# Attention over every 64th key: the order of the first four loads (Q block 0, keys, Q block 1, values)

## The chip, the cores and the metric

One core of one Trainium2 chip. Before the change: 130.33 us (130.28 to 130.64, 3 runs).

Names: PE is the matmul engine, ACT, DVE and POOL the three elementwise engines, SP the engine that issues the DMA transfers. A *piece* is one record of the trace that says when one of the 16 DMA engines moved one batch of bytes (256 bytes in the keys and values, 32 KB in the loads of Q, 8 KB in the stores), and how long that took. "Q 0" is short for Q block 0.

## The reference

```python
def setup_inputs():
    batch, heads, seq, dim = (8, 12, 1024, 64)      # Q, K, V: float32; stride: 64
def reference(Q, K, V, stride):
    scale = 1.0 / np.sqrt(dim)
    for i in range(seq):
        attend_positions = np.arange(0, seq, stride)            # 16 keys per head
        scores = np.einsum('bhqd,bhkd->bhqk', q, k) * scale
        weights = softmax(scores)                               # (shortened)
        result[:, :, i, :] = np.einsum('bhqk,bhkd->bhqd', weights, v)[:, :, 0, :]
```

Every query attends to the same 16 keys of its head. Q and the result are 25 MB each; the keys and values that are needed are 0.39 MB each, in rows of 256 bytes.

## The kernel before

The 96 heads are handled in 24 groups of 4. A group is one 1 MB load of Q, 16 transposes on PE with two copies on ACT, the scores, two exponentials on ACT, the sums and outputs on PE, a scaling on DVE, and one 1 MB store. Eleven Q buffers and nine output buffers let loads run far ahead of compute, and stores lag far behind it. All loads and stores are issued by SP on one queue:

```python
    nc.sync.dma_start(k_raw, _ap_with(K, kv_src))      # 1536 rows of 256 bytes
    nc.sync.dma_start(v_raw, _ap_with(V, kv_src))      # 1536 rows of 256 bytes
    ...
    def load(g):                                       # own form of the copy instruction
        qn[g] = qn_pool.tile([P, 32 * D], FP32, name="qn", tag="qn")
        _copy(nc, qn[g], _ap_with(Q, [[HG * SD // 32, 32], [1, HG * SD // 32]], g * HG * SD))
    for g in range(QBUFS):                             # QBUFS = 11
        load(g)
    ...
    nc.gpsimd.tensor_copy(out=v_bf, in_=v_raw)         # POOL, waits for the values
    ...
    for n in range(2):                                 # four value matmuls on PE;
        for c in range(2):                             # DVE spreads each into v_bd
            ...
    for g in range(2):                                 # PE: only now the first transposes
        for x in range(2):
            transposes(g, x)
    scores(0)
    for g in range(NG):
        ...                                            # sums, outputs, next scores and transposes
        store(g)
        if g + QBUFS < NG:
            load(g + QBUFS)
```

In PE's program order the transposes of Q block 0 stand behind the value matmuls, whenever Q block 0 arrives: in the trace of before it has landed at 8.8 us, and its first transpose starts at 14.29 us, after the last value matmul at 14.02.

The softmax here doesn't subtract the row's maximum and nothing guards it: scores larger than these inputs give would overflow.

## Time and profile before

| | before |
|---|---|
| time | 130.33 us |
| span of the profile | 128.5 us |
| DMA queue: first piece, last piece ended | 1.84, 127.08 us |
| compute: last instruction ended | 114.2 us |
| store 0 issued / first piece moved | 25.2 / 33.05 us |

The lines of the profile page that say what bounds the kernel: the span; the busy share of the DMA engines and the rate in 40 slices of 3.2 us; the DMA queue's packets, MB and share of 16 engines' time; and the shares of the chain of waits.

```profile
span 128.5 us, 2215 instructions
...
DMA  2999989999899899999999999999998999999980
GB/s 57 351 398 418 449 367 490 388 423 439 339 421 487 357 441 439 413 434 449 383 467 426 393 459 428 393 469 421 405 469 357 416 434 416 421 428 421 434 337 23
...
q1 hardware_dynamic: 7712, 51.12, 96.3%
...
ACT 60%; PE 13%; DVE 5%; DMA 3%; POOL 3%; issue 2%; ACTq 1%; DVEq 0%; POOLq 0%
```

The DMA share is 9 tenths or more from the second slice to the last but one, apart from single eights: the queue is the limit. The chain of waits names ACT, but that chain ends with the last compute instruction at 114.2 us; after that SP only waits for stores. The waits of SP (total us, times, longest us) show that end:

```profile
SPq L307 <- DMA out_dram<-out_sb: 12.6, 1, 12.6
```

The start, from the timeline (start, duration, engine, line, what, and in brackets the idle time before and who ended it):

```profile
0.73 0.44 SPq L89 DMA_DIRECT2D k_raw<-in_K_dram  x1
...
1.23 0.71 SPq L90 DMA_DIRECT2D v_raw<-in_V_dram  x1
...
1.99 12.62 SPq L34 DMA_DIRECT2D qn<-in_Q_dram  x11
...
5.06 1.60 POOL L116 CAST k_dup<-k_raw 128x768 bf16<-128x768 f32 x2 [3.04 <-DMA k_raw<-in_K_dram]
...
7.80 0.83 POOL L124 CAST v_bf<-v_raw 128x768 bf16<-128x768 f32 x1
...
14.29 1.91 PE L193 MATMUL qt_ps<-identity,qn 128*128 128x128 bf16 x16
...
25.18 0.63 SPq L34 DMA_DIRECT2D out_dram<-out_sb  x1
```

The keys' POOL cast starts at 5.06 us, the values' at 7.80, the first transpose at 14.29, and store 0 is issued at 25.18. The trace's pieces show one stream: keys and values from 1.84 to about 6 us, then Q blocks 0 to 10 back to back, then store 0 at 33.05. Between the issue of store 0 and its turn lie almost 8 us: compute has slack.

### The profile page before, as it was taken

The page shows a single profiled execution, that of the slowest core. Times are in us where ns is not written, and L with a number is a line of the kernel's source. Part 1 is how long each engine was busy: PE and PEld are TensorE (multiplying, and loading weights), DVE is VectorE, ACT ScalarE, POOL GpSimd, SP SyncE. Part 2 cuts the span into 40 slices and gives each one's busy share as a digit, 9 for nine tenths or more (in the row PEclk, how much of TensorE's full clock was granted, in tenths as well). Part 3 has the DMA queues.
Part 4 walks back from the last instruction along what each step waited for, and adds up shares of the span by engine and source line. Part 5 has one row for each costly group of instructions (what it writes and reads, how often), then busy time and mean ns, then how long its engine had stood idle before and what let it go on. Part 6 is the DMA issues. An engine that isn't in the chain of part 4 may idle for free.

```text
span 128.5 us, 2215 instructions
## 1 busy us (share of the span) xinstructions
PE 69.4 (54%) x880; PEld 51.1 (40%) x880; DVE 83.7 (65%) x144; ACT 86.3 (67%) x103; POOL 5.1 (4%) x23
## 2 busy tenths in 40 slices
PE   0071665975656866558766578665687655510000
PEld 0040542754445654445544456443465444300000
DVE  6229963787677777787777877877877778750000
ACT  2163294988889888898888898888988888400000
POOL 4470000000000000000000000000000000000000
PEclk9999997799999999999999999999999999955555
DMA  2999989999899899999999999999998999999980
GB/s 57 351 398 418 449 367 490 388 423 439 339 421 487 357 441 439 413 434 449 383 467 426 393 459 428 393 469 421 405 469 357 416 434 416 421 428 421 434 337 23
DMA packets 7722, 51.26 MB, mean 399 GB/s; under 512 B 3872, under 2 KB 3872, under 8 KB 3872
## 3 DMA queue, kind: packets, MB, share of 16 engines
q1 hardware_dynamic: 7712, 51.12, 96.3%
q8 instruction: 7, 0.11, 0.4%
q14 instruction: 3, 0.02, 0.0%
HBM read 25.95 MB, written 25.17 MB: 398 GB/s over the span
## 4 chain that ended last, share of the span: by engine, by line
ACT 60%; PE 13%; DVE 5%; DMA 3%; POOL 3%; issue 2%; ACTq 1%; DVEq 0%; POOLq 0%
ACT qt L198 34%; ACT w L218 26%; PE sc L206 8%; DVE v_bd L180 3%; DMA k_raw<-in_K_dram 3%; PE qt_ps L193 2%; PE o_ps L238 2%; DVE out_sb L243 1%; POOL k_dup L116 1%; POOL perm_v L120 1%; PE sm L227 1%; POOL v_bf L124 1%; ACTq L307 1%; DVEq L307 0%; PE vp L175 0%
## 5 line engine op out<-in xcount | busy, mean ns | idle before, releaser
L243 DVE TENSOR_TENSOR out_sb<-o_ps,rec 128x512 f32<-128x512 f32 x96 | 63.3, 688 | 15.3 <-PE o_ps L238 12.9
L198 ACT COPY qt<-qt_ps 128x1024 bf16<-128x1024 bf16 x48 | 46.2, 1015 | 5.2 <-PE qt_ps L193 4.7
L218 ACT ACTIVATE w<-sc 64x512 bf16<-64x512 f32 x48 | 35.4, 737 | 13.2 <-PE sc L206 12.9
L238 PE MATMUL o_ps<-v_bd,w 128*128 128x256 bf16 x192 | 33.4, 278 | 0.6 <-DVE out_sb L243 0.6
L193 PE MATMUL qt_ps<-identity,qn 128*128 128x128 bf16 x384 | 30.7, 227 | 0.2 <-ACT qt L198 0.2
L193 PEld LDWEIGHTS <-qn 128*128 128x128 bf16 x384 | 27.0, 102 | 3.9 <-issue 2.6
L206 PE MATMUL sc<-qt,k_t 128*32 128x512 bf16 x96 | 9.8, 395 | 24.5 <-ACT qt L198 24.5
L238 PEld LDWEIGHTS <-w 128*128 128x128 bf16 x192 | 14.3, 98 | 6.9 <-issue 6.2
L206 PEld LDWEIGHTS <-k_t 128*32 128x32 bf16 x96 | 4.4, 93 | 29.3 <-issue 29.2
L231 DVE RECIPROCAL rec<-sm 128x32 f32<-128x32 f32 x24 | 8.6, 358 | 9.0 <-PE sm L227 9.0
L227 PE MATMUL sm<-s_sel,w 128*128 128x4 bf16 x192 | 8.5, 166 | 6.9 <-ACT w L218 6.9
L227 PEld LDWEIGHTS <-w 128*128 128x128 bf16 x192 | 6.4, 96 | 11.0 <-ACT w L218 11.0
L180 DVE TENSOR_SCALAR v_bd<-vp,mask 128x384 bf16<-128x384 f32 x16 | 8.5, 608 | 0.1
L166 ACT CAST k_t<-kp 64x512 bf16<-64x512 f32 x6 | 3.5, 579 | 3.6 <-PE kp L160 3.5
L160 PE MATMUL kp<-perm_k,k_dup 128*128 128x128 bf16 x12 | 1.5, 312 | 6.7 <-POOL k_dup L116 6.7
L175 PE MATMUL vp<-v_bf,perm_v 128*128 128x384 bf16 x4 | 1.8, 490 | 4.6 <-DVE v_bd L180 4.1
L160 PEld LDWEIGHTS <-k_dup 128*128 128x128 bf16 x12 | 1.2, 145 | 6.7 <-POOL k_dup L116 6.7
L138 DVE TENSOR_SCALAR slot_i<-iota_p 128x1 int16<-128x1 int16 x1 | 0.2, 156 | 4.7 <-POOL iota_p L136 4.7
L166 ACT ACT_TABLE_LOAD x1 | 1.3, 1283 | 2.5 <-DVE k_t L127 2.5
L127 DVE MEMSET k_t<- 128x1536 uint32 x1 | 1.3, 1338 | 1.1 <-PEq L293 1.1
L175 PEld LDWEIGHTS <-perm_v 128*128 128x128 bf16 x4 | 0.5, 127 | 3.7 <-issue 3.7
L116 POOL CAST k_dup<-k_raw 128x768 bf16<-128x768 f32 x2 | 1.6, 827 | 3.0 <-DMA k_raw<-in_K_dram 3.0
(15 smaller groups left out, 6.0 us busy)
## 6 DMA issues: line engine op xcount, KB each, us to landing
qn<-in_Q_dram SPq DMA_DIRECT2D x24, 1024.0 KB, 19.0
out_dram<-out_sb SPq DMA_DIRECT2D x24, 1024.0 KB, 19.5
k_raw<-in_K_dram SPq DMA_DIRECT2D x1, 384.0 KB, 4.3
v_raw<-in_V_dram SPq DMA_DIRECT2D x1, 384.0 KB, 5.4
```

Of the source, the lines that this page charges most:

```text
L116: nc.gpsimd.tensor_copy(out=k_dup[:, :, e], in_=k_raw)
L160: nc.tensor.matmul(kp[:, i], lhsT=k_dup[:, 4 * n + i].rearrange("p e d -> p (e d)"), rhs=pk, start=True, stop=True,)
L166: nc.scalar.copy(k_t[h, 4 * n : 4 * n + 4, :, :, e].rearrange("p n c s k -> p (n c s) k"), kp[h].rearrange("p n c s k -> p (n c s) k"),)
L180: nc.vector.tensor_scalar(out=v_bd[:, 6 * n : 6 * n + 6, c, s], in0=vp, scalar1=mask[:, s : s + 1], scalar2=None, op0=ALU.mult,)
L193: nc.tensor.transpose(ps[:, i], _ap_with(qb, [qb.ap[0], [2, P]], extra_offset=(8 * x + i) * 2 * P + 1), identity,)
L198: nc.scalar.copy(qt[g][:, x], ps)
L206: nc.tensor.matmul(sc[32 * j : 32 * j + 32], lhsT=kt[:, 32 * j : 32 * j + 32], rhs=_ap_with(q, [q.ap[0], [P, 8], [8 * P, 2], [1, 32]], ext ...
L218: nc.scalar.activation(out=_ap_with(wa, [wa.ap[0], [P, 8], [1, 2], [2, 32]], extra_offset=64 * a), in_=sc[64 * a : 64 * a + 64].rearrange( ...
L227: nc.tensor.matmul(sm[:, :, i], lhsT=wt[g][:, i], rhs=s_sel, start=True, stop=True)
L231: nc.vector.reciprocal(rec[g], sm.rearrange("p b i e -> p b (i e)"))
L238: nc.tensor.matmul(ps[:, :, i], lhsT=wt[g][:, 2 * c + i], rhs=v_bd[:, g // 2, g % 2].rearrange("p s d -> p (s d)"), start=True, stop=True,)
L243: nc.vector.tensor_tensor(out=out_sb[g][:, :, 4 * c : 4 * c + 4], in0=ps.rearrange("p b i (e d) -> p b (i e) d", e=2), in1=rec[g][:, :, 4 ...
```

## The change

Its intent is to have Q block 0 on the chip sooner, since compute starts with it. No byte and no instruction is added; only the order of SP's first four loads changes.

```diff
--- before.py
+++ after.py
@@ -86,8 +86,6 @@
     k_raw = const.tile([P, NC, D], FP32, name="k_raw")
     v_raw = const.tile([P, NC, D], FP32, name="v_raw")
     kv_src = [[stride * D, P], [2 * HG * SD, NC], [1, D]]
-    nc.sync.dma_start(k_raw, _ap_with(K, kv_src))
-    nc.sync.dma_start(v_raw, _ap_with(V, kv_src))
 
     qn = {}
 
@@ -99,6 +97,10 @@
 
     for g in range(QBUFS):
         load(g)
+        if g == 0:
+            nc.sync.dma_start(k_raw, _ap_with(K, kv_src))
+        elif g == 1:
+            nc.sync.dma_start(v_raw, _ap_with(V, kv_src))
 
 
     identity = const.tile([P, P], BF16, name="identity")
```

## The prediction

> **What bounds the kernel now.** The DMA queue, not an engine. By the DMA share per slice and the one-microsecond windows, the 16 DMA engines are full from about 3 us to 124 us; the queue table gives 96.3%. The transfer records show one first-in-first-out stream: keys and values (256-byte pieces) move from 1.84 to 6.05 us, Q block 0 lands at about 8.8 us, Q blocks 0 to 10 are followed at once by store 0, which begins at 33.05 us, and the last piece of store 23 ends at 127.1 us of the 128.5 us span. This agrees with the Trainium skill, "DMA: Bandwidth & Descriptors", section "Queues, rings and completion order": each engine consumes its ring in order.
>
> Compute is a second, shorter chain. The chain of waits says ACT 60%, but that chain ends at 114.2 us. In it ACT runs without a gap from 26 to 110 us, about 3.94 us a group, never waiting for Q. The last 12.6 us is SP waiting for stores.
>
> **What the change does.** It adds and removes no bytes and no instruction: on PE, DVE, ACT and POOL the order is the same, only SP's first four loads are permuted. On the queue Q 0 goes before the keys, Q 0 and Q 1 before the values. The intent, Q sooner, gains nothing: PE reads Q 0 first at 14.3 us, 5 us after it landed, because in PE's program order the transposes stand behind the four value matmuls, the last of which waits for DVE's v_bd (9.68 to 14.0 us).
>
> Costs (estimates from these durations): a Q block moves in 2.48 us (spacing of Q starts), keys or values in about 2. Keys should land near 7.5 us instead of 5.0, values near 11.7 instead of 6.6. The POOL cast of the values (now at 7.80) then starts near 11.8: +4.0 us. Everything behind it, v_bd, transposes, first exponential, store 0, moves by that: store 0 from 25.2 to about 29.2 us, end of compute from 114.2 to about 118.2.
>
> **On the critical path.** Almost nothing. The queue holds loads until 33.05 us, so store 0 issued at 29.2 (about 1.1 us from issue to first piece) comes in time; slack today is about 6.7 us, about 2.7 would be left. At the end store 23 would be issued near 118.3 and its turn comes at 122.3. The DMA stream stays gapless and ends at the same time. A small gain is possible: the first half of the keys took 1.4 us against 0.7 for later equal pieces; Q 0 in front may hide this. The final wait of SP should shrink from 12.6 to about 8.6 us.
>
> **Predicted:** 130.1 us, range 129.4 to 131.0 (8 in 10). Chances: faster by over 2% 0.02, within 2% 0.94, slower by over 2% 0.04.
>
> **What would show each step.** Right: K lands 2 to 3 us and V 4.5 to 5.5 us later; the first transpose near 18.3 us; store 0 issued near 29 us; DMA share still 0.9 or more in the slices from 26 to 36 us; last compute near 118 us; span 127.7 to 129. Wrong: a slice under 0.8 around 30 to 36 us would mean that the slack was used up.
>
> **What would make it wrong.** The small key and value pieces could move slower when mixed between the 32 KB pieces, delaying values by more than 6.7 us in all and opening a hole in the stream before store 0; or the one DMA engine that finishes 2 us after the others (127.1 against 125) may lag more or less.

## More of the kernel before

The metric is the device time of one execution in microseconds (us); a kernel's time is the median of its runs.

The view in stretches (length, busy time of each engine, PE clock, DMA share, GB/s; each piece is counted whole where it starts; one round of 16 pieces of 32 KB more or less at an edge is 33 GB/s in a stretch of 16 us, and 7 GB/s in one of 80 us):

```profile
core 0: us, PE busy (x) PEld busy (x) DVE busy (x) ACT busy (x) POOL busy (x), PEclk, DMA share, GB/s
0.00:16.00 16.00, 4.71 (x32) 3.47 (x33) 9.78 (x21) 5.37 (x8) 5.08 (x23) 1.00 0.94 334
16.00:32.00 16.00, 11.20 (x130) 8.03 (x128) 10.89 (x20) 12.73 (x16) 0.00 (x0) 0.89 1.01 421
32.00:112.00 80.00, 53.08 (x718) 39.52 (x719) 60.85 (x103) 68.16 (x81) 0.00 (x0) 1.00 1.00 422
112.00:128.50 16.50, 0.38 (x2) 0.10 (x1) 2.23 (x4) 0.00 (x0) 0.00 (x0) 0.53 0.79 330
```

From 16 to 112 us the stream runs at 421 to 422 GB/s; slower are only the opening and the last stretch, in which the stores run out. The Trainium skill, "HBM Reference", section "Specifications (TRN2)", says that a core which streams alone reaches about 425 GB/s; this trace agrees.

## The result, and the profile after

The changed kernel takes 131.13 us (130.95 to 131.39, 6 runs) against 130.51 us of before (130.28 to 130.64, 6 runs): ratio 1.0053, 95% interval 1.0038 to 1.0067. (Ratios here are the mean time of one kernel's fast runs over that of the other's of the same rounds, so not quite the ratio of the medians.) Run once more later, it came to 131.26 us, ratio 1.0069 (1.0056 to 1.0082). It is slower by a little, and clearly so: 131.13 lies just outside the predicted range of 129.4 to 131.0.

The page after:

```profile
span 129.2 us, 2215 instructions
...
DMA  5799999999899899999999999999999999999970
GB/s 162 234 388 373 426 446 426 386 426 421 360 444 467 375 444 446 388 449 431 393 472 426 388 467 411 406 467 391 421 441 391 413 429 416 434 416 431 413 330 23
...
q1 hardware_dynamic: 7712, 51.12, 96.2%
...
ACT 59%; PE 14%; DVE 5%; DMA 5%; issue 4%; POOL 2%; POOLq 1%; ACTq 1%; DVEq 0%; SPq 0%
```

The middle is as full as before, and there is no hole near 33 us, where store 0 comes in. The timeline of the start:

```profile
0.74 0.58 SPq L34 DMA_DIRECT2D qn<-in_Q_dram  x1
...
1.37 0.56 SPq L101 DMA_DIRECT2D k_raw<-in_K_dram  x1
1.99 0.93 SPq L34 DMA_DIRECT2D qn<-in_Q_dram  x1
...
2.96 0.59 SPq L103 DMA_DIRECT2D v_raw<-in_V_dram  x1
3.60 11.72 SPq L34 DMA_DIRECT2D qn<-in_Q_dram  x9
8.07 1.60 POOL L118 CAST k_dup<-k_raw 128x768 bf16<-128x768 f32 x2 [6.05 <-DMA k_raw<-in_K_dram]
...
12.40 0.83 POOL L126 CAST v_bf<-v_raw 128x768 bf16<-128x768 f32 x1 [1.52 <-DMA v_raw<-in_V_dram]
...
18.90 1.91 PE L195 MATMUL qt_ps<-identity,qn 128*128 128x128 bf16 x16
...
29.84 0.63 SPq L34 DMA_DIRECT2D out_dram<-out_sb  x1
...
30.57 0.55 SPq L34 DMA_DIRECT2D qn<-in_Q_dram  x1
```

The casts of keys and values start 3.0 and 4.6 us later (8.07 and 12.40 instead of 5.06 and 7.80), the first transpose 4.6 us later, store 0 was issued at 29.84 instead of 25.18, and compute ended near 119.2 instead of 114.2 us. (The values themselves landed 5.7 us later, at about 12.4 instead of 6.6 us; before, their cast stood behind other POOL work when they came.) SP's last wait shrank by nearly as much, as it should if late compute costs nothing:

```profile
SPq L309 <- DMA out_dram<-out_sb: 8.4, 1, 8.4
```

The stretches say where the time went:

```profile
0.00:16.00 16.00, 2.26 (x14) 1.55 (x15) 5.18 (x12) 4.76 (x7) 5.16 (x23) 1.00 0.92 313
16.00:32.00 16.00, 11.64 (x97) 8.03 (x97) 11.49 (x22) 9.05 (x11) 0.00 (x0) 1.00 1.01 423
32.00:112.00 80.00, 54.05 (x739) 40.64 (x737) 61.32 (x102) 69.20 (x83) 0.00 (x0) 1.00 1.00 423
112.00:128.50 16.50, 3.10 (x36) 1.84 (x36) 5.85 (x11) 3.30 (x4) 0.00 (x0) 0.75 0.82 343
```

From 16 to 112 us the rate is that of before (423 and 423 against 421 and 422 GB/s). The first 16 us are not: 313 GB/s instead of 334. Part of that gap is the edge at 16 us. With each piece spread evenly over its own duration the rates are 300 and 315 GB/s, and the difference, 0.24 MB, is 0.56 us of the later stream. What is missing there is moved at the end (343 instead of 330 in the last stretch).

The pieces give the same in time. The columns are the start of the first piece, the mean start of the 32 pieces of Q block 3 (by then keys, values and Q blocks 0 to 2 are through in either order), the mean start of the 128 pieces of store 23, and the end of the last piece, all in us:

```
                 first   Q block 3   store 23   last end
before            1.84     14.01      123.76     127.08
changed           2.10     14.57      124.32     127.74
difference       +0.27     +0.56       +0.56      +0.66
```

The stream is 0.56 us behind when Q block 3 starts, and as much at store 23, 110 us later. The loss happens in the opening of the stream and is never won back, since the stream has no gap in which it could be.

### The profile page after: what moved, and what is told of

It is laid out like the page before. It is cut to its first block, busy times and chain, and to the rows that moved or that the text cites. A ratio compares the mean times of both kernels' runs of the same rounds, so it can differ in the third digit from the quotient of the medians.

```text
span 129.2 us, 2215 instructions
## 1 busy us (share of the span) xinstructions
PE 71.1 (55%) x880; PEld 52.1 (40%) x880; DVE 83.8 (65%) x144; ACT 86.3 (67%) x103; POOL 5.2 (4%) x23
## 4 chain that ended last, share of the span: by engine, by line
ACT 59%; PE 14%; DVE 5%; DMA 5%; issue 4%; POOL 2%; POOLq 1%; ACTq 1%; DVEq 0%; SPq 0%
ACT qt L200 33%; ACT w L220 26%; PE sc L208 8%; DMA k_raw<-in_K_dram 5%; DVE v_bd L182 3%; PE qt_ps L195 3%; PE o_ps L240 2%; DVE out_sb L245 1%; POOL k_dup L118 1%; POOL perm_v L122 1%; PE sm L229 1%; POOLq L309 1%; ACTq L309 1%; DVEq L309 0%; SPq L34 0%
## 5 line engine op out<-in xcount | busy, mean ns | idle before, releaser
L240 PE MATMUL o_ps<-v_bd,w 128*128 128x256 bf16 x192 | 33.9, 281 | 0.6 <-DVE out_sb L245 0.6
L195 PE MATMUL qt_ps<-identity,qn 128*128 128x128 bf16 x384 | 31.6, 231 | 0.2 <-ACT qt L200 0.2
L195 PEld LDWEIGHTS <-qn 128*128 128x128 bf16 x384 | 27.6, 104 | 3.9 <-issue 2.6
```

Of the source, the lines that this page charges most:

```text
L195: nc.tensor.transpose(ps[:, i], _ap_with(qb, [qb.ap[0], [2, P]], extra_offset=(8 * x + i) * 2 * P + 1), identity,)
L240: nc.tensor.matmul(ps[:, :, i], lhsT=wt[g][:, 2 * c + i], rhs=v_bd[:, g // 2, g % 2].rearrange("p s d -> p (s d)"), start=True, stop=True,)
```

## The experiments

Three theories. **A**: what comes first in the stream sets the loss; opening with Q is dearer than opening with keys. **B**: each change between 256-byte and 32 KB pieces costs something; before has one such change, the changed kernel four. **C**: late compute costs it after all, at store 0 or at the last stores. Eleven runs were made, all correct. Each ratio is against runs of the kernel before on the same chip.

### e1: keys, Q 0, values, Q 1

```diff
-    nc.sync.dma_start(v_raw, _ap_with(V, kv_src))
 ...
         load(g)
+        if g == 0:
+            nc.sync.dma_start(v_raw, _ap_with(V, kv_src))
```

> Order keys, Q 0, values, Q 1: the keys open the stream as before, only the values are moved. Theory A (the loss of about 0.6 us is the opening of the stream by a 32 KB piece instead of 256-byte pieces): time within 0.15 us of before (ratio 1.000 to 1.001), first piece at 1.84 us. Theory B (the loss is paid at each change between small and large pieces; before has 1 change, the changed kernel 4, this one 3): about +0.4 us, ratio 1.003.

Measured: 130.70 us against 130.58, ratio 1.001 (0.999 to 1.003). Its first stretch:

```profile
0.00:16.00 16.00, 2.78 (x16) 1.70 (x17) 7.85 (x17) 4.76 (x7) 5.17 (x23) 1.00 0.92 334
```

334 GB/s, as before; Q block 3's pieces start at 14.00 us on the mean (before: 14.01). Three changes between large and small pieces cost nothing that can be seen. That speaks against B.

### e2 and e3: Q 0, keys, values, Q 1, and Q 0, Q 1, keys, values

```diff
     for g in range(QBUFS):
         load(g)
+        if g == 0:        # e3: if g == 1
+            nc.sync.dma_start(k_raw, _ap_with(K, kv_src))
+            nc.sync.dma_start(v_raw, _ap_with(V, kv_src))
```

> Order Q 0, keys, values, Q 1: Q 0 opens the stream, but keys and values stay together (2 changes between small and large pieces). Theory A (opening): the whole loss stays, +0.6 us, ratio 1.004 to 1.006. Theory B (changes): a third of it, about +0.2 us, ratio 1.0015.

> Order Q 0, Q 1, keys, values. As the run before this one for theories A and B (A +0.6 us, B +0.2 us). Values land as late as in the changed kernel (about 11.8 us), keys about 2.5 us later than there; if the late keys mattered (theory C: late compute), this would be the slowest of the three by some tenths of a us.

Measured: e2 131.17 us, ratio 1.0048 (1.0028 to 1.0067); e3 131.18 us, ratio 1.0050 (1.0033 to 1.0068). The first stretch of e2:

```profile
0.00:16.00 16.00, 2.74 (x15) 1.66 (x16) 6.90 (x15) 4.76 (x7) 5.11 (x23) 1.00 0.94 311
```

And the same stretch of e3:

```profile
0.00:16.00 16.00, 2.25 (x14) 1.55 (x15) 4.37 (x10) 4.46 (x7) 5.11 (x23) 1.00 0.94 311
```

Both run at 311 GB/s there, and Q block 3 starts at 14.56 and 14.59 us. All three orders that begin with Q 0 lose the same; e1, whose values stand behind Q 0 as well, but whose keys go first, loses nothing. A holds and B falls.

### e4: compute late, loads as before

```diff
+    idle = const.tile([P, NC, D], BF16, name="idle")
+    for _ in range(6):                                   # e5: 15
+        nc.gpsimd.tensor_copy(out=idle, in_=k_raw)
     v_bf = const.tile([P, NC, D], BF16, name="v_bf")
     nc.gpsimd.tensor_copy(out=v_bf, in_=v_raw)
```

> The loads in the order of before, but six idle POOL copies of about 0.8 us ahead of the cast of the values, so that compute starts about 4.7 us later, as in the changed kernel, with the load order of before. Theories A and B: no loss, within 0.15 us of before, last compute near 119 us. Theory C (the late compute itself costs the 0.6 us, by store 0 or by the last stores): the loss of the changed kernel, +0.6 us, ratio 1.005.

Measured: 130.61 us against 130.58, ratio 1.001 (0.999 to 1.0029). The cast of the values and the issue of store 0:

```profile
13.07 0.83 POOL L127 CAST v_bf<-v_raw 128x768 bf16<-128x768 f32 x1
...
30.08 0.63 SPq L34 DMA_DIRECT2D out_dram<-out_sb  x1
```

Compute is 5.3 us late, more than in the changed kernel, and the time is that of before. Its first stretch is that of before, too:

```profile
0.00:16.00 16.00, 2.26 (x14) 1.55 (x15) 4.51 (x10) 4.77 (x7) 10.03 (x29) 1.00 0.95 336
```

C falls for a delay of this size.

### e5: how far the slack reaches

The same with fifteen idle copies.

> Load order of before, fifteen idle POOL copies instead of six: six had moved the cast of the values by 5.3 us, so fifteen should move it by about 13 us. Model of two chains (queue and compute, slack 6.7 us ahead of store 0): store 0 is issued near 38.4 us, the queue has run dry at about 33.3, a hole of about 6.2 us appears in the DMA slices between 33 and 40 us, and the time rises by about 6.2 us to 136.7 (ratio about 1.048). If compute had no such slack limit (the queue bound by bytes alone, however late the stores), the time would stay within 0.3 us.

Measured: 138.67 us against 130.38, ratio 1.0634 (1.0620 to 1.0647), so +8.3 us where 6.2 were expected. The stretches about the hole:

```profile
34.00:39.00 5.00, 4.96 (x47) 3.62 (x48) 3.30 (x6) 2.94 (x4) 0.00 (x0) 1.00 0.02 3
39.00:42.00 3.00, 2.80 (x36) 1.90 (x35) 2.69 (x5) 2.39 (x4) 0.00 (x0) 1.00 0.86 306
42.00:46.00 4.00, 2.64 (x39) 1.98 (x36) 3.00 (x5) 3.40 (x5) 0.00 (x0) 1.00 1.05 295
46.00:50.00 4.00, 2.71 (x40) 2.04 (x37) 3.00 (x5) 3.47 (x5) 0.00 (x0) 1.00 1.00 426
```

The hole is there: 3 GB/s from 34 to 39 us. Compute was 13.2 us late (cast of the values at 20.98 us), and from the mean end of Q 10's last pieces (33.2 us) to the first piece of store 0 (39.69) the engines stood still for about 6.4 us, which is the sum expected. The other 1.9 us came after it. By mean starts, against before, store 0 is 6.4 us late, the load behind it (Q 11) 7.5, store 1 8.3, and all that follows 8.2 to 8.3. In the stretch from 42 to 46 us the stream moved only 295 GB/s, and the first 16 pieces of the load behind store 0 took 1.4 to 2.9 us each instead of the usual 1.22. A load that meets a stream just set going is slow here as well as in the opening; the store's own first pieces took the usual 0.31 us. Why that is so is not shown.

### e6: Q 0 in 8 KB pieces

```diff
-            nc, qn[g], _ap_with(Q, [[HG * SD // 32, 32], [1, HG * SD // 32]], g * HG * SD)
+            nc, qn[g],
+            _ap_with(Q, [[HG * SD // (128 if g == 0 else 32), 128 if g == 0 else 32],
+                         [1, HG * SD // (128 if g == 0 else 32)]], g * HG * SD),
```

> The changed kernel's order, with Q 0 alone read in 8 KB pieces (128 rows) instead of 32 KB pieces. Theory A1 (the opening is dear because each engine's first piece is large and its filling is not overlapped): the loss falls from 0.6 to 0.3 us or less. Theory A2 (opening with Q costs the same whatever its pieces, because the keys' and values' small pieces make use of a slow start that Q does not): loss stays 0.5 to 0.6 us.

Measured: 131.30 us against 130.38, ratio 1.0068 (1.0056 to 1.0080). The size of the first pieces is not the cause (A1 falls). The pieces show a small gain (Q block 3 at 14.44 us instead of 14.57), but the time shows none. The first 16 pieces of 8 KB are slow, too: 0.58 us on the mean instead of the usual 0.31.

### e7: a small transfer as opener

```diff
+    warm = const.tile([16, NC, D], FP32, name="warm")
+    nc.sync.dma_start(warm, _ap_with(K, [[stride * D, 16]] + kv_src[1:]))
     for g in range(QBUFS):
         load(g)
```

> The changed kernel's order with one extra transfer ahead of Q 0: 16 key rows of 12 pieces, 192 pieces of 256 bytes, into a tile that nobody reads. It costs one more issue on SP (0.4 to 0.6 us before Q 0 is issued) and about 0.2 us of the engines. Theory A1 (opening with small pieces is what counts): the loss falls to 0.2 to 0.4 us in spite of the extra transfer. Theory A2: the loss stays 0.6 us or rises to 0.8.

Measured: 131.77 us against 130.38, ratio 1.0101 (1.0086 to 1.0115). This is worse than either theory expected. The time is 0.5 to 0.6 us above the changed kernel's 131.13 and 131.26, and by the pieces the stream is 0.75 us behind the changed kernel's (Q block 3 at 15.32 us). Q 0 was issued 0.46 us later (1.19 instead of 0.74), and its first 16 pieces still took 1.75 us on the mean. So a few small pieces win nothing back; they put off the issue of Q 0, which is 0.46 of the 0.75 us, and add work of their own.

### e8: keys and values on two queues

```diff
     nc.sync.dma_start(k_raw, _ap_with(K, kv_src))
-    nc.sync.dma_start(v_raw, _ap_with(V, kv_src))
+    nc.scalar.dma_start(v_raw, _ap_with(V, kv_src))
```

> The order of before, but the values are issued by ACT on its own queue at the same moment as the keys by SP, a try for a faster opening: Q 0 is issued 0.7 us earlier on SP and keys and values generate their pieces side by side. If the slow feed between 1.84 and 2.75 us (3 to 6 of 16 engines at work in before) is a limit of one issuing queue, the opening gets about 0.3 us shorter: 130.2 us, ratio 0.998. If it is the start of the engines themselves, no gain: ratio 1.000.

Measured: 130.26 us against 130.38, ratio 1.0002 (0.9986 to 1.0018). In its trace Q block 3 starts 0.14 us sooner than before (13.87 us). If that is a gain, it is too small for these rounds. Keys and values did not open the stream side by side: both were issued at 0.73 us, but the keys' first piece moved at 1.84 us and the values' at 3.03. So the expected test of one issuing queue against two was not quite made. It was the one try for a version better than both kernels, and it is not shown to be one.

### e9, e10, e11: Q 0 beside the keys, Q 0 in the plain form, and the changed kernel again

```diff
     def load(g):
         qn[g] = qn_pool.tile([P, 32 * D], FP32, name="qn", tag="qn")
+        if g == 0:        # e9: nc.scalar.dma_start, e10: nc.sync.dma_start
+            nc.sync.dma_start(qn[g], _ap_with(Q, [[HG * SD // P, P], [1, HG * SD // P]]))
+            return
         _copy(...)
```

Both on top of the changed kernel's order. The kernel's own copy instruction goes through a symbolic description of both sides; the plain form is what keys and values use. e11 is the changed kernel without any edit.

> The changed kernel's order, but Q 0 is issued by ACT on its own queue at the same moment as the keys by SP, in 8 KB pieces. If the loss is that an opening with Q alone leaves the first microsecond of the stream unused, while the keys' small pieces use it (some 300 of 3072 pieces were through by 2.75 us in before) and start 0.27 us sooner, then keys beside Q 0 should win it back: mean start of Q 3's pieces near 14.0 us as before, time within 0.2 us of before (ratio 1.000 to 1.0015), although values still come after Q 1. If any order with Q 0 at the front is dear, the loss stays 0.5 to 0.9 us.

> The changed kernel's order; Q 0 alone is issued in the form the keys use (plain copy of 128 rows) instead of the kernel's own form. The issue of Q 0 took SP 0.58 us against 0.43 for the keys, and its first piece came 1.37 us after the issue's start against 1.11. If the form of the instruction makes that difference, the issue shrinks to about 0.44, the first piece comes at 1.84, and the loss against before falls to about 0.3 us; if it is the transfer itself, issue 0.58 and loss 0.6 to 0.9 us (the 8 KB pieces alone had given 0.9).

> The changed kernel once more, on the chip of these runs, to be compared with the two others directly: 0.6 us over before (ratio 1.004 to 1.006).

Measured, against 130.37 us in the same rounds: e9 131.20 us, ratio 1.0065 (1.0051 to 1.0079); e10 130.90 us, ratio 1.0038 (1.0026 to 1.0050); e11 131.26 us, ratio 1.0069 (1.0056 to 1.0082).

The issue of Q 0 in the timeline of e6 (own form, 8 KB pieces):

```profile
0.73 0.59 SPq L34 DMA_DIRECT2D qn<-in_Q_dram  x1
```

The same in e10 (plain form, 8 KB pieces):

```profile
0.73 0.39 SPq L95 DMA_DIRECT2D qn<-in_Q_dram  x1
```

The plain form takes SP 0.39 us instead of 0.59, and the first piece of Q 0 moves at 1.76 us instead of 2.10. Q block 3 starts at 14.21 us instead of 14.44, and the time falls by 0.4 us (130.90 against 131.26 of e11, whose interval does not meet e10's; e11 still has the 32 KB pieces, but e6 had shown no change of time from these). So the form of Q 0's instruction makes up some 0.23 us of the stream's 0.56, and by time 0.4 us of e11's 0.9; the rest stays with the plain form.

e9 is a miss, and its edit did not do what it was meant to do. ACT and SP issued Q 0 and the keys both at 0.73 us, but Q 0's pieces began at 1.89 us and the keys' at 2.50; one small piece had started by 2.75 us and 100 of 3072 by 5.0. So the keys never ran beside the opening of Q 0, and what they would have done there is untested: e9 is one more order with Q 0 in front. It was to win back nearly all and its timed runs won nothing; its profiled run, in which Q block 3 starts at 14.21 us, was also its fastest by 0.4 us (130.66; the others 131.06 to 131.44), so the trace does not show what the slower runs did.

### All orders side by side

In us, from the pieces of the profiled runs:

```
                         first   Q block 3   store 23   last end
before  K V Q0 Q1         1.84     14.01      123.76     127.08
e4      K V Q0 Q1, late   1.83     14.02      123.76     127.27
e1      K Q0 V Q1         1.83     14.00      123.79     127.65
changed Q0 K Q1 V         2.10     14.57      124.32     127.74
e11     Q0 K Q1 V         2.10     14.60      124.35     128.13
e2      Q0 K V Q1         2.09     14.56      124.29     127.86
e3      Q0 Q1 K V         2.09     14.59      124.37     127.90
e6      Q0 (8 KB) K Q1 V  2.10     14.44      124.21     128.02
e10     Q0 (plain) K Q1 V 1.76     14.21      123.98     127.65
e9      Q0 (ACT) K Q1 V   1.89     14.21      123.96     127.44
e7      small Q0 K Q1 V   1.77     15.32      125.06     128.67
e8      K V (ACT) Q0 Q1   1.84     13.87      123.63     127.64
```

Keys in front: 14.00 to 14.02 (13.87 in e8). Q 0 in its own form in front: 14.44 to 14.60; in the plain form 14.21, twice. The rates of the first 16 us, counted with each piece spread over its duration, say the same: 314 to 315 GB/s in before, e1 and e4, 300 in the changed kernel, e2 and e3. The shift at Q block 3 is the shift at store 23 to within 0.03 us in each. The last end scatters more: the last DMA engine ends 3.3 to 4.0 us after the mean start of store 23, with no clear relation to the order of the loads (3.3 in before, 3.9 in e1, whose time is that of before). This scatter goes into the time: in every one of these profiled runs the time is 3.2 to 3.4 us more than the last end. That may be why the times of the changed kernel lie between 0.6 and 0.9 us over before, when its stream is 0.56 to 0.58 us behind; one profile for each kernel does not settle it.

### What makes the opening dear, and what stays open

In before, 263 of the 3072 small pieces had started by 2.75 us (249 had ended), when the stream came to full width; that is about 0.25 us of work at the 1.06 pieces a nanosecond at which the next 1.4 us went. So before did as much as a stream that starts at 2.50 us at full speed. With Q 0 in front no piece had ended by then: the first 16 pieces of Q 0 began at 2.10 to 2.69 us and took 1.84 us on the mean, instead of the 1.22 that such a piece takes later. Counted back in the same way, at the later 421 GB/s, from what had moved by 5.0 us (845 kB, each piece spread evenly over its duration), the changed kernel did as much as a stream that starts at full speed at 2.99 us; e6 (886 kB) at 2.90, e10 (987 kB) at 2.66. These estimates lie 0.49, 0.40 and 0.16 us after that of before, and Q block 3 was 0.56, 0.43 and 0.20 us late. By this estimate nearly all of the loss is there before the first key has moved (at 5.0 to 5.2 us in these three). Of the changed kernel's 0.56 us, 0.27 stands already at the first piece (2.10 instead of 1.84 us). Behind keys and values, first large pieces took 1.53 us in before (Q 0) and 1.31 and 1.49 in the changed kernel (Q 1 and Q 2), so something is lost there in both orders. This account of the opening by pieces fits the sum, but it is argued from the records, not isolated: a small opener (e7) did not help, smaller pieces (e6) helped the stream by 0.13 us and the time not at all, the plain form did in part (e10), and e9 did not bring the keys beside Q 0. Shown are the place of the loss (the opening), its cause in the order (Q 0 in front) and the share of the instruction's form. Open is why the first pieces of Q 0 are slow.

## Why the prediction was wrong

- **"The DMA queue, not an engine" bounds the kernel: right.** e4 delays compute by 5.3 us for nothing, e5 shows the limit of the slack.
- **"No bytes and no instruction", compute +4.0 us, store 0 at 29.2 us, last compute at 118.2 us: right, a little small.** The values were put at 11.7 us and landed at about 12.4; their cast moved by 4.6 us, store 0 to 29.84, the last compute to about 119.2. ("ACT runs without a gap" was misread: it was busy for 68.16 of the 80 us from 32 to 112, and waited for the scores 23 times. Nothing rested on it.) The final wait of SP was put at 8.6 us and measured 8.4.
- **"The DMA stream stays gapless": right.** There is no slice under 0.8 near 33 us, and the rate from 16 us on is that of before.
- **"and ends at the same time. A small gain is possible: ... Q 0 in front may hide this": this step failed.** The stream's opening was taken as a constant, or as a cost of the keys that Q 0 might hide. It is a term of the sum, and Q 0 in front moves it the other way: with Q 0 in front the stream is 0.56 us behind when Q block 3 starts (14.57 against 14.01 us), and stays behind. The slow first half of the keys was read as waste that Q 0 could hide; in fact Q 0's own opening is the dearer one: counted back at full speed, the stream starts at about 2.99 us with Q 0 in front and at about 2.50 with the keys in front.
- **The risks named** (a hole ahead of store 0; a last engine that lags) were not it. The lag of the last engine scatters by some tenths of a microsecond, without following the order, and may have widened the loss in some runs.

"Within 2%" came true; the number missed its range by 0.13 us because the range left no room for a dearer opening.

## What to carry to other kernels

In a kernel that is bound, like this one, by one gapless DMA stream, ask of an order of loads what it does to the stream itself: its opening, its holes and its end. Getting Q 0 on the chip sooner was worth nothing here, since PE's program order kept it waiting, and the start of the stream deserves its own line in the estimate, since a loss there stays to the end. To measure such a term, compare the mean start of one fixed transfer behind the reordered part: it showed 0.56 us cleanly, where the end of the run scattered by as much as that.

## What the Trainium skill lacked or had wrong

- "DMA: Bandwidth & Descriptors", section "Latency and other measured facts", gives about 600 ns to the first byte for transfers issued by SP. Counted from the start of the issue to the first piece, the runs show 1.11 us (keys), 1.37 us (Q 0 in the kernel's own form), 1.03 us (Q 0 in the plain form) and 1.28 us (store 0 after the hole in e5). The page may count from another moment; it does not say.
- No page says that the first large pieces of a load which opens a stream are slow: 1.84 us on the mean for 32 KB instead of 1.22 (for 8 KB in e6 0.58 instead of 0.31), and 1.4 to 2.9 us for the first load after a hole (e5), while a store's first pieces took the usual 0.31 us.
- No page says that two forms of the same copy differ at the issue: SP took 0.59 us for the own form and 0.39 us for the plain one, for the same 8 KB pieces (e6, e10), and the time differed by 0.4 us (on two chips, on which before took 130.38 and 130.37 us).
- "DMA: Bandwidth & Descriptors", section "Why small descriptors are slow (HBM only)", reckons 11 cycles instead of 8 for a 256-byte piece, which as an estimate is 73% of the full rate. Here the keys' pieces went at up to 1.14 a nanosecond, 292 GB/s, which is 69% of the 421 GB/s of the later stream, and at 1.06 a nanosecond over 1.4 us, which is 64%. That is a little less than the reckoning, in which a second cost that the page names, 32 bytes of descriptor metadata for each transfer, is not counted; no run here separates the two.
